# VectorE copies the mixer's R, the last taps, tables and memory are queued later, transposes of queries move by one product, the final scaling runs on three engines

## The chip, the cores and the metric

The kernel runs on one core of a Trainium2 chip, as one launch. The metric is the device time of that launch in microseconds. Engines are named as in the profile: PE is the matrix engine (TensorE), PEld its weight loads, DVE is VectorE, ACT is ScalarE, POOL is GpSimd, and SP (SyncE) issues most DMAs.

## The reference

Two layers over 512 tokens of width 1024, all in float32. Each layer is a half-step SwiGLU FFN (hidden width 2816), a mixer of three groups of heads (gated causal convolution of 31 taps with LayerNorm and silu, sliding-window attention, attention to 256 memory tokens), a second half-step FFN, and a final norm:

```python
for l in range(DEPTH):
    h = x + 0.5 * swiglu(rms_norm(x, ffn1_norm[l]), ffn1_w1[l], ffn1_w3[l], ffn1_w2[l])
    n = rms_norm(h, mix_norm[l])
    u_conv, q, k, v, q_mem = jnp.split(n @ w_in[l], splits, axis=-1)
    y_conv = conv_module(u_conv, conv_w[l], conv_b[l], conv_ln_g[l], conv_ln_b[l])
    q = apply_rope(rms_norm(q, swa_q_norm[l]), cos, sin)
    k = apply_rope(rms_norm(k, swa_k_norm[l]), cos, sin)
    y_swa = sliding_window_attention(q, k, v, swa_sinks[l])
    mk, mv = jnp.split(rms_norm(mem, mem_norm[l]) @ w_mem_kv[l], 2, axis=-1)
    y_mem = memory_attention(rms_norm(q_mem, mem_q_norm[l]), rms_norm(mk, mem_k_norm[l]), mv)
    h = h + jnp.concatenate([y_conv, y_swa, y_mem], axis=-1) @ w_out[l]
    h = h + 0.5 * swiglu(rms_norm(h, ffn2_norm[l]), ffn2_w1[l], ffn2_w3[l], ffn2_w2[l])
    x = rms_norm(h, final_norm[l])
```

## The kernel before

**Layout.** Activations lie transposed: the residual `h` is 8 blocks of 128 channels by 512 tokens. RMS norms need sums over channels, so squares are added up on ACT and DVE, and PE sums them over partitions (`col_sums`, a matmul with a column of ones per 128 tokens); `rms_cols` makes the factor per token (POOL's power in `rsq`), and `spread` turns it into a 128x512 tile `R` with the same value on all partitions, by four matmuls. `kept` copies that tile from PSUM to SBUF.

**Precision by three products.** Every large product is done three times in a reduced format: each operand is split into a high and a low part (`hi`, `lo`), and `mm3` multiplies hi by hi, lo by hi and hi by lo (lines 174 to 176). A weight tile is loaded raw (512 KB for 1024 columns, three `raw` buffers, four `whi`/`wlo` pairs). Then ACT writes hi (line 143) and DVE writes lo as raw minus hi (line 144): that is `split`, one DVE operation of 1.2 us a tile. The other way is `split_by_dma`: ACT writes hi and minus hi (lines 148, 149), and a DMA issued by POOL adds the raw weight from HBM onto it (line 150). `weights(..., on)` chooses: V is the first way, G the second.

**FFN.** `ffn` computes the first four of 22 hidden units plainly (`up`, whose weights are chosen between the two ways), and the others in pairs with a scheme of seven products (`Seven`, `up_pair`), which needs sums of operands and weights on DVE (`msum`, line 298; `raw`, line 363). The hidden units are used in four quarters of 6, 6, 6 and 4; after each, eight output blocks are accumulated and added to `h` (line 460). In the first FFN of a layer, a function `aside` is called after quarter 0: `prepare(l)`, which makes the rope tables (layer 0 only, some sixty small DVE operations, lines 475 to 514), this layer's tables `cg`, `sg` and `gmem` (lines 556 to 559), and the memory tokens' keys and values (`memory`, a product of 48 matmuls with its own weights, operand splits at line 154, and four weight tiles).

**Mixer.** The input projection is a sequence of products, written in a string `ORDER`: `c00` to `c21` are the six halves of the convolution's GLU, `q0` to `q3` the queries and keys of 128 tokens each, `Q0` to `Q3` their transposes to columns, `v`, `V` the same for values and memory queries, `a` the attention, `t0` to `t2` the taps of three blocks of convolution channels (31 DVE operations each), `s` its LayerNorm and swish. Then the output projection has two phases: first the five blocks of attention for all eight outputs, then the three of the convolution. `a` runs the last convolution half inside.

**Order.** Tile's scheduler decides each engine's order of instructions from the program's order, priorities and its own model of time. `tc.issue_after(x)`, used by `queued()`, tells it to place instructions behind x; it adds no semaphore. All engines work through their queues in order, so an instruction that waits holds up what is behind it.

**Tail.** After the last FFN, `spread` of the last factor stays in PSUM, DVE scales eight 128x512 blocks by it and by the final gain (line 975), and SP writes each block out (line 976).

Of the kernel before, what the change touches and what calls it, by code (L numbers as in the profile page):

```python
# [10 lines left out]
F32 = mybir.dt.float32  # L11
# [7 lines left out]
P = 128  # L19
D = 1024  # L20
# [25 lines left out]

ORDER = "c00 c01 q0 c10 q1 Q0 c11 q2 Q1 v0 q3 Q2 v1 v2 Q3 V0 v3 V1 c20 V2 V3 a t0 t1 t2 s"

# [13 lines left out]
def trunk(ctx: ExitStack, tc: tile.TileContext, xT, memT, pos, w1a, w3a, w2a, w1b, w3b, w2b,  # L62
# [131 lines left out]
    def col_sums(st, tag="cf"):  # L194

        ss = bank([P, 4], tag)
        for t in range(st.n // P):
            for i, x in enumerate(st.sums):
                tail[0] = T.matmul(ss[:, t : t + 1], x[:, blk(t)], onec, start=i == 0, stop=i == len(st.sums) - 1)
        return ss  # L200
# [13 lines left out]

    def kept(pr, tag):
        R = res.tile([P, S], F32, tag=tag, name=tag)
        A.activation(R, pr, AF.Copy)
        return R
# [180 lines left out]
    def ffn(l, w13, w2, x, sums, factors, last, at_product, aside=None):  # L399
# [38 lines left out]
        for q, (f0, nf) in enumerate(QUARTERS):  # L438
# [14 lines left out]
            for d in range(KD):  # L453
                while len(begun) < (d + 1 if ahead or d else 3):
                    with nullcontext() if ahead or d else queued():
                        begin(len(begun))
                ps, w = begun[d]
                for j in range(nf - 2, nf):
                    mm3(ps, at(w, ALL, blk(j)), g[f0 + j], False, j == nf - 1)
                V.scalar_tensor_tensor(out=h[:, d, :], in0=ps, scalar=0.5, in1=h[:, d, :], op0=ALU.mult, op1=ALU.add)  # L460
                if not ahead:
                    last(d)
            if aside and not q:
                aside()

# [141 lines left out]
    def mixer(l, x, st, last):  # L607
# [32 lines left out]
        def conv_half(c, i):  # L640
            nonlocal R
            ps = bank([P, S], "po") if c == 2 else mm()
            with queued():
                project(ps, weights(wconv[l, c, i], 1024, G if c else V, spare() if c == 2 else None), x)
            if c == 0:
                with queued():
                    if i == 0:
                        V.tensor_copy(rc, rms_cols(st, D))
# [142 lines left out]
        def scaled(kind, b, po):  # L791
# [10 lines left out]
            z = ring("yn")[:, 0 : n * HD]  # L802
            V.tensor_tensor(out=heads(z), in0=po[:, :, 0:HD], in1=rd.unsqueeze(2).to_broadcast([P, n, HD]), op=ALU.mult)
            return z

        def attended(kind, b, z):
# [58 lines left out]
        def taps(c):  # L865
            V.tensor_scalar(out=cv[:, c, :], in0=ypad[:, c, 0:S], scalar1=conv_w[:, c, 0:1], scalar2=conv_b[:, c : c + 1],
                            op0=ALU.mult, op1=ALU.add)
            for j in range(1, TAPS):
                V.scalar_tensor_tensor(out=cv[:, c, :], in0=ypad[:, c, j : j + S], scalar=conv_w[:, c, j : j + 1],  # L869
                                       in1=cv[:, c, :], op0=ALU.mult, op1=ALU.add)  # L870

# [51 lines left out]
    for l in range(L):  # L923
# [44 lines left out]
        else:  # L968
            def last(d):
                st.add(h[:, d, :], last=d == KD - 1)  # L970

            ffn(l, (w1b, w3b), w2b, nxt.x, sums, factors, last, 1)
            pr = spread(rms_cols(st, D))
            for d in range(KD):
                V.scalar_tensor_tensor(out=h[:, d, :], in0=h[:, d, :], scalar=fin[:, d : d + 1], in1=pr, op0=ALU.mult, op1=ALU.mult)
                nc.sync.dma_start(out[:, d, :], h[:, d, :])
# [58 lines left out]
```

## Time and profile before

| | before |
|---|---|
| time, median of 3 | 1820.17 us (1819.33 to 1820.87) |
| the profiled execution | 1818.45 us |
| its span on the core | 1816.7 us |
| mean granted PE clock | 0.996 |
| DMA traffic | 250.45 MB, mean 138 GB/s |

Each execution's time includes 1.75 us around the span that the profile shows. The page gives the busy time of each engine; the windows give PE's idle time by place. In layer 0 the first FFN runs to about 380 us, the mixer to about 570, and the second FFN follows; layer 1 starts near 910, its mixer near 1270. A row of a timeline has the start, the duration, engine, line, operation, names, shapes, and in brackets the idle time before it and what ended it.

### The profile page before, as it was taken

Reading aid. Unit: us, or ns where it says so; the run is one execution under the profiler, and the core shown is the slowest. Engines: PE = TensorE matmul, PEld = TensorE weight load, DVE = VectorE, ACT = ScalarE, POOL = GpSimd, SP = SyncE. Lnnn points to the kernel's source line nnn. Section 1 sums busy time; section 2 is a strip of 40 time slices with the busy share of each in tenths; the row PEclk is TensorE's granted clock in tenths of the full one; section 3 lists DMA queues with packets and bytes.
Section 4 is the critical chain, followed back from the end, with each engine's and each line's share of the span. In section 5 each row is a group of like instructions: output and inputs, shape, how many; then the busy total and the mean of one; then the engine's idle time right before and its main releaser. Section 6 shows DMA issues by size and latency. Waiting matters only on the chain.

```text
span 1816.7 us, 28098 instructions
## 1 busy us (share of the span) xinstructions
PE 1763.6 (97%) x10996; PEld 1578.3 (87%) x10996; DVE 1281.8 (71%) x1902; ACT 899.6 (50%) x1367; POOL 192.3 (11%) x207
## 2 busy tenths in 40 slices
PE   8999999999999999999999999999989999999997
PEld 6889999878788989898888898988777879898986
DVE  8967666569947857575678675766698567675755
ACT  4545444364746535353655453535456555353532
POOL 2001000025111000000010010000350010000000
PEclk9999999999999999999999999999999999999998
DMA  7456655173148456565565475643640566474622
GB/s 245 109 169 172 169 136 152 53 215 80 36 98 208 107 144 168 142 164 140 155 137 156 144 176 141 169 119 98 170 103 16 146 158 161 131 182 120 167 78 81
DMA packets 93589, 250.45 MB, mean 138 GB/s; under 512 B 9616, under 2 KB 11920, under 8 KB 93456
## 3 DMA queue, kind: packets, MB, share of 16 engines
q1 hardware_dynamic: 77040, 190.45, 34.2%
q0 software_dynamic: 16416, 58.20, 17.7%
q8 instruction: 86, 1.41, 0.3%
q14 instruction: 47, 0.39, 0.1%
HBM read 246.52 MB, written 2.10 MB: 137 GB/s over the span
## 4 chain that ended last, share of the span: by engine, by line
PE 75%; DVE 12%; issue 6%; DMA 4%; ACT 2%; SPq 0%; POOLq 0%; DVEq 0%; POOL 0%; ACTq 0%
PE mm L174 10%; PE mm L175 10%; PE mm L176 10%; PE po L174 8%; PE po L176 8%; PE po L175 8%; PE pt L175 6%; PE pt L174 6%; PE pt L176 6%; DVE there L869 5%; DVE wlo L144 1%; DMA raw<-in_wvm 1%; DMA raw<-in_wconv 1%; DVE nmw L760 1%; PE cf L174 1%
## 5 line engine op out<-in xcount | busy, mean ns | idle before, releaser
L143 ACT ACTIVATE whi<-raw 128x1024 fp32r<-128x1024 f32 (+3 forms) x368 | 339.2, 925 | 481.8 <-PE mm L175 233.4
L144 DVE TENSOR_TENSOR wlo<-raw,whi 128x1024 fp32r<-128x1024 f32 (+3 forms) x368 | 388.9, 1058 | 156.2 <-ACT whi L143 154.9
L175 PE MATMUL mm<-glo,whi 128*128 128x512 f32 x752 | 293.7, 391 | 0.0
L176 PE MATMUL mm<-ghi,wlo 128*128 128x512 f32 x752 | 292.6, 389 | 0.0
L174 PE MATMUL mm<-ghi,whi 128*128 128x512 f32 x752 | 290.8, 391 | 0.7 <-ACT ghi L143 0.7
L176 PE MATMUL po<-mh,wlo 128*128 128x256 f32 x864 | 244.6, 283 | 1.4 <-DVE wlo L144 1.4
L174 PE MATMUL po<-mh,whi 128*128 128x256 f32 x864 | 244.8, 283 | 0.8 <-ACT part L382 0.8
L174 PE MATMUL pt<-xhi,whi 128*128 128x256 f32 x864 | 243.2, 283 | 2.4 <-ACT xhi L143 2.0
L175 PE MATMUL pt<-xlo,whi 128*128 128x256 f32 x864 | 243.8, 283 | 1.5 <-DVE xlo L144 1.5
L175 PE MATMUL po<-ml,whi 128*128 128x256 f32 x864 | 244.6, 283 | 0.0
L176 PE MATMUL pt<-xhi,wlo 128*128 128x256 f32 x864 | 243.7, 283 | 0.0
L460 DVE SCALAR_TENSOR_TENSOR h<-mm,h 128x512 f32<-128x512 f32 x128 | 87.8, 689 | 137.3 <-PE mm L176 137.3
L174 PEld LDWEIGHTS pt<-xhi,whi 128*128 128x128 f32 x864 | 165.1, 192 | 3.9 <-ACT xhi L143 2.4
L175 PEld LDWEIGHTS pt<-xlo,whi 128*128 128x128 f32 x864 | 165.7, 192 | 2.5 <-DVE xlo L144 1.7
L174 PEld LDWEIGHTS mm<-ghi,whi 128*128 128x128 f32 x752 | 141.2, 188 | 30.2 <-ACT ghi L143 1.2
L174 PEld LDWEIGHTS po<-mh,whi 128*128 128x128 f32 x864 | 165.8, 192 | 1.8 <-ACT part L382 1.2
L176 PEld LDWEIGHTS po<-mh,wlo 128*128 128x128 f32 x864 | 165.8, 192 | 1.6 <-DVE wlo L144 1.6
L176 PEld LDWEIGHTS mm<-ghi,wlo 128*128 128x128 f32 x752 | 141.3, 188 | 29.8 <-issue 0.5
L175 PEld LDWEIGHTS po<-ml,whi 128*128 128x128 f32 x864 | 165.8, 192 | 0.6
L175 PEld LDWEIGHTS mm<-glo,whi 128*128 128x128 f32 x752 | 141.3, 188 | 28.3 <-issue 0.5
L176 PEld LDWEIGHTS pt<-xhi,wlo 128*128 128x128 f32 x864 | 165.5, 192 | 0.0
L869 DVE SCALAR_TENSOR_TENSOR there<-ypad,par,there 128x512 f32<-128x512 f32 x180 | 135.7, 762 | 1.4
(304 smaller groups left out, 3280.2 us busy)
## 6 DMA issues: line engine op xcount, KB each, us to landing
raw<-in_w2a SPq DMA_DIRECT2D x48, 384.0 KB, 3.6
raw<-in_w2b SPq DMA_DIRECT2D x48, 384.0 KB, 3.5
raw<-in_w1b SPq DMA_DIRECT2D x26, 512.0 KB, 3.6
raw<-in_w3b SPq DMA_DIRECT2D x26, 512.0 KB, 3.9
raw<-in_w1a SPq DMA_DIRECT2D x25, 512.0 KB, 3.6
raw<-in_w3a SPq DMA_DIRECT2D x25, 512.0 KB, 3.9
wsum<-in_w1a SPq DMA_DIRECT2D x18, 512.0 KB, 4.3
wsum<-in_w3a SPq DMA_DIRECT2D x18, 512.0 KB, 4.4
```

The source lines that it names most:

```text
L143: A.activation(hi, x, AF.Copy)
L144: on.tensor_tensor(out=lo, in0=x, in1=hi.bitcast(F32), op=ALU.subtract)
L174: T.matmul(ps, a[0], b[0], start=first, stop=False, **more)
L175: T.matmul(ps, a[0], b[1], start=False, stop=False, **more)
L176: tail[0] = T.matmul(ps, a[1], b[0], start=False, stop=last, **more)
L460: V.scalar_tensor_tensor(out=h[:, d, :], in0=ps, scalar=0.5, in1=h[:, d, :], op0=ALU.mult, op1=ALU.add)
L760: V.tensor_reduce(out=each(nmw, i), in_=pp[i], axis=AX.X, op=ALU.max)
L869: V.scalar_tensor_tensor(out=cv[:, c, :], in0=ypad[:, c, j : j + S], scalar=conv_w[:, c, j : j + 1], in1=cv[:, c, :], op0=ALU.mult, op1=AL ...
```

## The change

Eight edits in one diff:

1. `ORDER` moves the transposes `Q0`, `Q1`, `Q2` one product later.
2. `col_sums` runs over the partial sums first and over the tokens' blocks inside, so that products of the first partial sum need not wait for the second.
3. In the mixer, DVE instead of ACT copies `R`.
4. In the mixer, half `c10` of the convolution has its weight split on DVE and not by DMA.
5. In layer 0's first FFN, unit 3 of the plain units has its two weights split by DMA and not on DVE.
6. `aside` (tables and memory) is placed behind the eighth addition to `h` of quarter 0.
7. The last ten taps of the last channel block are placed behind the last scaling of window attention.
8. The final scaling: ACT multiplies by the gain as each block of `h` is done, and the factor per token is spread, copied (ACT) and multiplied (DVE) by blocks of 128 tokens for six of the eight channel blocks, with one output DMA each; POOL multiplies the other two.

```diff
-ORDER = "c00 c01 q0 c10 q1 Q0 c11 q2 Q1 v0 q3 Q2 v1 v2 Q3 V0 v3 V1 c20 V2 V3 a t0 t1 t2 s"
+ORDER = "c00 c01 q0 c10 q1 c11 Q0 q2 v0 Q1 q3 v1 Q2 v2 v3 Q3 V0 V1 c20 V2 V3 a t0 t1 t2 s"
...
         ss = bank([P, 4], tag)
-        for t in range(st.n // P):
-            for i, x in enumerate(st.sums):
-                tail[0] = T.matmul(ss[:, t : t + 1], x[:, blk(t)], onec, start=i == 0, stop=i == len(st.sums) - 1)
+
+        for i, x in enumerate(st.sums):
+            for t in range(st.n // P):
+                tail[0] = T.matmul(ss[:, t : t + 1], x[:, blk(t)], onec, start=i == t == 0, stop=i == len(st.sums) - 1, skip_group_check=True)
...
-    def kept(pr, tag):
+    def kept(pr, tag, on=A):
         R = res.tile([P, S], F32, tag=tag, name=tag)
-        A.activation(R, pr, AF.Copy)
+        if on is A:
+            A.activation(R, pr, AF.Copy)
+        else:
+            on.tensor_copy(R, pr)
         return R
...
-            project(ps, weights(w13[i][l, f], 1024, V if f == 0 or l == 0 and w13[0] is w1a else G), x)
+            project(ps, weights(w13[i][l, f], 1024, V if f == 0 or f < 3 and l == 0 and w13[0] is w1a else G), x)
...
-                V.scalar_tensor_tensor(out=h[:, d, :], in0=ps, scalar=0.5, in1=h[:, d, :], op0=ALU.mult, op1=ALU.add)
+                added = V.scalar_tensor_tensor(out=h[:, d, :], in0=ps, scalar=0.5, in1=h[:, d, :], op0=ALU.mult, op1=ALU.add)
                 if not ahead:
                     last(d)
             if aside and not q:
-                aside()
+                with tc.issue_after(added.ins):
+                    aside()
...
-                project(ps, weights(wconv[l, c, i], 1024, G if c else V, spare() if c == 2 else None), x)
+                project(ps, weights(wconv[l, c, i], 1024, V if c + i < 2 else G, spare() if c == 2 else None), x)
...
-                        R = kept(spread(rc), "R")
+                        R = kept(spread(rc), "R", V)
...
-            V.tensor_tensor(out=heads(z), in0=po[:, :, 0:HD], in1=rd.unsqueeze(2).to_broadcast([P, n, HD]), op=ALU.mult)
+            scaling[kind] = V.tensor_tensor(out=heads(z), in0=po[:, :, 0:HD], in1=rd.unsqueeze(2).to_broadcast([P, n, HD]), op=ALU.mult)
...
             for j in range(1, TAPS):
-                V.scalar_tensor_tensor(out=cv[:, c, :], in0=ypad[:, c, j : j + S], scalar=conv_w[:, c, j : j + 1],
-                                       in1=cv[:, c, :], op0=ALU.mult, op1=ALU.add)
+
+                with tc.issue_after(scaling["w"].ins) if c == CC - 1 and j > 2 * TAPS // 3 else nullcontext():
+                    V.scalar_tensor_tensor(out=cv[:, c, :], in0=ypad[:, c, j : j + S], scalar=conv_w[:, c, j : j + 1],
+                                           in1=cv[:, c, :], op0=ALU.mult, op1=ALU.add)
...
                 st.add(h[:, d, :], last=d == KD - 1)
+                A.activation(h[:, d, :], h[:, d, :], AF.Copy, scale=fin[:, d : d + 1])
...
-            pr = spread(rms_cols(st, D))
-            for d in range(KD):
-                V.scalar_tensor_tensor(out=h[:, d, :], in0=h[:, d, :], scalar=fin[:, d : d + 1], in1=pr, op0=ALU.mult, op1=ALU.mult)
+            r = rms_cols(st, D)
+            R = res.tile([P, S], F32, tag="R", name="R")
+            k = KD - 2
+            for t in range(NT):
+                pr = bank([P, P], ("mm", "po")[t % 2])
+                T.matmul(pr, r[:, t : t + 1].to_broadcast([P, P]), ident, start=True, stop=True)
+                A.activation(R[:, blk(t)], pr, AF.Copy)
+                z = h[:, 0:k, blk(t)]
+                V.tensor_tensor(out=z, in0=z, in1=R[:, blk(t)].unsqueeze(1).to_broadcast([P, k, P]), op=ALU.mult)
+                nc.sync.dma_start(out[:, 0:k, blk(t)], z)
+            for d in range(k, KD):
+                G.tensor_tensor(out=h[:, d, :], in0=h[:, d, :], in1=R, op=ALU.mult)
                 nc.sync.dma_start(out[:, d, :], h[:, d, :])
```

The first place is DVE's queue at the end of quarter 0 in layer 0's first FFN. Line 460 (464 in the changed kernel) is the addition to `h`, one for each of eight outputs; lines 154 and 144 with `raw`, `gn` and 128x1024 are memory's operand and weight splits. Before:

```order
L154 SCALAR_TENSOR_TENSOR wlo_1270<-raw_1267,gn_80,whi_1269 128x256 x4
L460 SCALAR_TENSOR_TENSOR h_79<-mm_1134,h_79 128x512
L144 TENSOR_TENSOR wlo_1291<-raw_1292,whi_1290 128x1024
L242 TENSOR_TENSOR st_1273<-st_1273,sq_1332 128x256
L242 TENSOR_TENSOR st_1273<-st_1273,sq_1337 128x256
L242 TENSOR_TENSOR st_1273<-st_1273,sq_1342 128x256
L242 TENSOR_TENSOR st_1273<-st_1273,sq_1347 128x256
L460 SCALAR_TENSOR_TENSOR h_79<-mm_1160,h_79 128x512
L144 TENSOR_TENSOR wlo_1309<-raw_1310,whi_1308 128x1024
L460 SCALAR_TENSOR_TENSOR h_79<-mm_1186,h_79 128x512
L154 SCALAR_TENSOR_TENSOR wlo_1329<-raw_1326,gn_80,whi_1328 128x256 x4
```

and in the changed kernel:

```order
L464 SCALAR_TENSOR_TENSOR h_79<-mm_1162,h_79 128x512
L464 SCALAR_TENSOR_TENSOR h_79<-mm_1188,h_79 128x512
L488 CAST pf_1208<-posi_102 128x4
L565 TENSOR_TENSOR gmem_125<-rw_100 128x64
L154 SCALAR_TENSOR_TENSOR wlo_1272<-raw_1269,gn_80,whi_1271 128x256 x2
L246 TENSOR_TENSOR st_1275<-st_1275,sq_1279 128x256
L154 SCALAR_TENSOR_TENSOR wlo_1272<-raw_1269,gn_80,whi_1271 128x256 x2
L144 TENSOR_TENSOR wlo_1293<-raw_1294,whi_1292 128x1024
L144 TENSOR_TENSOR wlo_1311<-raw_1312,whi_1310 128x1024
L489 TENSOR_TENSOR ypad_108<-cst_96,pf_1208 128x128
```

The first half of memory's splits (`wlo_1270`, `wlo_1291`, `wlo_1309`) stood ahead of the eighth addition; now the same splits (`wlo_1272`, `wlo_1293`, `wlo_1311`) stand behind it, with the rope table's operations after them. In layer 1 the same place of the changed kernel reads:

```order
L464 SCALAR_TENSOR_TENSOR h_79<-mm_9733,h_79 128x512
L561 TENSOR_TENSOR cg_123<-cs_114,rw_100 128x4x64
L563 SCALAR_TENSOR_TENSOR sg_124<-sn_115,rw_100 128x4x32 x2
L561 TENSOR_TENSOR cg_123<-cs_114,rw_100 128x4x64
L563 SCALAR_TENSOR_TENSOR sg_124<-sn_115,rw_100 128x4x32 x2
L565 TENSOR_TENSOR gmem_125<-rw_100 128x64
L154 SCALAR_TENSOR_TENSOR wlo_9765<-raw_9762,gn_80,whi_9764 128x256 x4
L144 TENSOR_TENSOR wlo_9775<-raw_9776,whi_9774 128x1024
```

Layer 1's six table operations, which DVE did during layer 0's mixer before, now stand between the addition and the first split. On PE, the memory product's place has not moved: it follows the quarter's last product directly in both kernels, and in the changed kernel (layer 0) its first instructions are:

```order
L176 MATMUL mm_1188<-ghi_749,wlo_1183 128x512
L174 MATMUL cf_1267<-whi_1292,whi_1271 128x512
L174 MATMUL mm_1268<-whi_1292,whi_1271 128x512
L175 MATMUL cf_1267<-wlo_1293,whi_1271 128x512
L176 MATMUL cf_1267<-whi_1292,wlo_1272 128x512
```

Two of them use high parts only; the third reads `wlo_1293`.

The second place is PE's queue in layer 0's mixer, at the transposes of the first queries (`Q0`, lines 566 and 571, from the tile `query`). Before:

```order
L174 MATMUL mm_3938<-ghi_3857,xhi_3582 128x512
L175 MATMUL mm_3938<-glo_3858,xhi_3582 128x512
L176 MATMUL mm_3938<-ghi_3857,xlo_3583 128x512
L566 MATMUL pt_3979<-cst_96,query_3744 128x128 x4
L174 MATMUL mm_3986<-xhi_3582,whi_3987 128x512
```

and in the changed kernel:

```order
L174 MATMUL mm_3980<-xhi_3584,whi_3981 128x512
L175 MATMUL mm_3980<-xlo_3585,whi_3981 128x512
L176 MATMUL mm_3980<-xhi_3584,wlo_3982 128x512
L571 MATMUL pt_4015<-cst_96,query_3746 128x128 x4
L174 MATMUL mm_4022<-ghi_3838,xhi_3584 128x512
```

The transposes stood behind the product of `q1` and now stand behind the next one, that of `c11`.

The third place is DVE's queue at the end of layer 0's attention; line 869 (878) is a tap, lines 798 to 803 (803 to 808) are the scaling of one block's attention, line 881 (890) begins the swish. Before:

```order
L869 SCALAR_TENSOR_TENSOR there<-ypad,par,there 128x512 x2
L144 TENSOR_TENSOR glo<-pt,ghi 128x128
L746 TENSOR_REDUCE nmr<-mm 128x2
L746 TENSOR_REDUCE nmr<-cf 128x2
L144 TENSOR_TENSOR glo<-pt,ghi 128x2x128
L747 SCALAR_TENSOR_TENSOR nmr<-nmr,rm 128x4
L144 TENSOR_TENSOR glo<-pt,ghi 128x2x128
L798 TENSOR_TENSOR rd_4772<-po,esw 128x2x3
L799 RECIPROCAL rd_4772<-rd_4772 128x6
L803 TENSOR_TENSOR aux_3741<-po,rd_4772 128x384
L801 RECIPROCAL rd_4794<-po 128x4
```

and in the changed kernel:

```order
L808 TENSOR_TENSOR aux_3743<-po,rd_4773 128x384
L878 SCALAR_TENSOR_TENSOR there<-ypad,par,there 128x512 x2
L806 RECIPROCAL rd_4795<-po 128x4
L878 SCALAR_TENSOR_TENSOR there<-ypad,par,there 128x512
L808 TENSOR_TENSOR aux_3743<-po,rd_4795 128x256
L144 TENSOR_TENSOR glo<-pt,ghi 128x128
L878 SCALAR_TENSOR_TENSOR there<-ypad,par,there 128x512
L144 TENSOR_TENSOR glo<-pt,ghi 128x2x128
L878 SCALAR_TENSOR_TENSOR there<-ypad,par,there 128x512
L144 TENSOR_TENSOR glo<-pt,ghi 128x2x128
L878 SCALAR_TENSOR_TENSOR there<-ypad,par,there 128x512 x5
```

Ten taps, which were spread among attention's operations before, come after the last window scaling (384 columns wide), between and behind the last splits of the attention's output.

More of the change, by code (lines that the diff above doesn't have):

```diff
@@ L802, in scaled @@
             z = ring("yn")[:, 0 : n * HD]
-            V.tensor_tensor(out=heads(z), in0=po[:, :, 0:HD], in1=rd.unsqueeze(2).to_broadcast([P, n, HD]), op=ALU.mult)
+            scaling[kind] = V.tensor_tensor(out=heads(z), in0=po[:, :, 0:HD], in1=rd.unsqueeze(2).to_broadcast([P, n, HD]), op=ALU.mult)
             return z
+        scaling = {}
         def attended(kind, b, z):
```

## The prediction

> **What bounds the kernel now.** I read the page first for who is busy, then its chain, then the matrix engine's waits, then windows around the waits.
>
> ```profile
> PE 1763.6 (97%) x10996; PEld 1578.3 (87%) x10996; DVE 1281.8 (71%) x1902; ACT 899.6 (50%) x1367; POOL 192.3 (11%) x207
> ...
> PE 75%; DVE 12%; issue 6%; DMA 4%; ACT 2%; SPq 0%; POOLq 0%; DVEq 0%; POOL 0%; ACTq 0%
> ```
>
> PE is the bound: 1763.6 of the span's 1816.7 us. The change adds and removes no large product, so only the 53.1 us in which PE stands still, and stretches at a low clock, are to be won. In the chain that ended last DVE is the next engine with 12%. So the reader is to look for where PE's idle time lies, and what DVE did before it.
>
> ```profile
> 60.00:80.00 20.00, 16.51 (x135) 1.00 0.62 167
> 130.00:150.00 20.00, 20.00 (x105) 1.00 0.42 132
> ...
> 380.00:510.00 130.00, 117.92 (x690) 0.99 0.36 88
> ...
> 1270.00:1410.00 140.00, 127.49 (x737) 1.00 0.40 98
> 1800.00:1816.70 16.70, 5.30 (x31) 0.67 0.34 126
> ```
>
> In each window the columns are its length, PE's busy time, the granted clock, DMA's share and GB/s. The two mixers hold 12.1 and 12.5 us of idle time, the first FFN's start 3.5, the tail 11.4. Between 130 and 150, where the memory tokens are projected in layer 0, PE never stops; that row matters below. The waits say who ended the idle time (total, count, longest).
>
> ```profile
> PE pt L566 <- DVE query L542: 5.0, 4, 1.3
> PE cf L176 <- DMA wlo<-in_wconv: 3.2, 2, 1.6
> PE pt L566 <- DVE query L690: 3.0, 2, 1.5
> ...
> PE pt L174 <- ACT xhi L143: 2.0, 1, 2.0
> PE pt L175 <- DVE xlo L144: 1.5, 1, 1.5
> PE cf L199 <- ACT sq L230: 1.4, 1, 1.4
> ```
>
> **First FFN, layer 0.** The waits of 2.0 and 1.5 us are both in the window 60 to 80: ACT and PE wait for sums that DVE makes late.
>
> ```profile
> 69.22 1.28 DVE L298 TENSOR_TENSOR msum<-n 128x512 f32<-128x512 f32 x2
> ```
>
> DVE has no gap around it. Among what it does before are the rope table's small operations and the fourth unit's weight splits:
>
> ```profile
> L144 DVE TENSOR_TENSOR wlo<-raw,whi 128x1024 fp32r<-128x1024 f32 x9 | 10.8, 1213 | 0.0
> ...
> L480 DVE SCALAR_TENSOR_TENSOR ypad<-ypad 128x128 f32<-128x128 f32 x4 | 1.1, 280 | 0.0
> ```
>
> The order of the changed kernel has no rope operation in this stretch, and the two splits of the fourth unit go to ACT with an accumulating DMA. Two splits at 1.2 and about ten small operations at 0.2 to 0.28 take some 4.5 us off DVE ahead of the sum, more than the 3.5 us of stall. **Gain 3.5**, bounds 2 to 3.5. The way by DMA is longer, and hidden by an early load:
>
> ```profile
> 34.22 1.06 ACT L143 ACTIVATE whi<-raw 128x1024 fp32r<-128x1024 f32 x1 [2.54 <-DMA raw<-in_w1a]
> ```
> ```profile
> 47.23 0.39 PE L174 MATMUL mm<-xhi,whi 128*128 128x512 f32 x1
> ```
>
> The fourth unit's first tile is there at 34.2, and PE comes to it at 47.2: 13 us for two copies of 1.06, an issue of 0.9 and a landing. Without that cover the loss would be like the 1.6 of the convolution's wait above.
>
> **Memory projection, both layers: the new wait.** `aside` is now queued behind the eighth h addition of quarter 0 (the first pieces of the order above). Before, its weight splits ran while PE was still in the quarter's last products:
>
> ```profile
> 132.14 1.22 DVE L144 TENSOR_TENSOR wlo<-raw,whi 128x1024 fp32r<-128x1024 f32 x1
> 135.34 0.69 DVE L460 SCALAR_TENSOR_TENSOR h<-mm,h 128x512 f32<-128x512 f32 x1 [1.98 <-PE mm L176]
> 135.94 1.66 DVE L154 SCALAR_TENSOR_TENSOR wlo<-raw,gn,whi 128x256 fp32r<-128x256 f32 x4
> ```
> ```profile
> 134.91 0.39 PE L176 MATMUL mm<-ghi,wlo 128*128 128x512 f32 x1
> 135.14 0.39 PE L174 MATMUL cf<-whi 128*128 128x512 f32 x1
> 135.37 0.39 PE L175 MATMUL cf<-wlo,whi 128*128 128x512 f32 x1
> ```
>
> PE went from the quarter's last product (134.91) into the memory product (135.14) without a gap, and its second instruction already reads a wlo. In the changed order PE still does exactly this, but now that wlo's split stands behind the h addition, which itself waits for the last product. From the addition's start DVE needs 0.60 (start to start, 135.34 to 135.94), some 0.3 for two small operations, 1.66 for the four scaled splits, one square sum (about 0.4) and 1.22 for the weight: the wlo is there 4.2 us after 135.34. PE can do two matmuls that need no wlo, until 135.6. It waits about 4.0. Then memory's second half: DVE has the rope's small operations between, about 7.1 us of work from the first weight's split to the third's, against 5.4 us of PE work (24 matmuls at 0.227 from start to start): 1.7 more. Layer 0 pays 5.7. In layer 1 there is no rope, but six table operations stand ahead of the splits, which the trace shows in the mixer:
>
> ```profile
> 440.24 0.28 DVE L558 SCALAR_TENSOR_TENSOR sg<-sn,rw 128x128 f32<-128x128 f32 x1
> ...
> 441.18 0.41 DVE L556 TENSOR_TENSOR cg<-cs,rw 128x256 f32<-128x256 f32 x1
> ```
>
> Two of 0.33 and four of 0.2 from start to start are 1.5 us in place of the square sum and the cast, so the first wait is about 4.8. The second half's raw tiles can only load when the first half's are split, which adds about half a microsecond: 5.2. **Loss 10.9 together.** Bounds 8 (only the first waits, DVE's small operations overlapping better) and 15 (below). Afterwards DVE has about 70 us of work in the next quarter's 76 us of PE time, so the lag is worked off without a second stall.
>
> PE's clock may fall after such a gap. The trace has this once:
>
> ```profile
> 433.29 0.44 PE L566 MATMUL pt<-cst,query 128*128 128x128 f32 x1 [1.24 <-DVE query L542]
> ...
> 434.50 0.52 PE L174 MATMUL mm<-whi,xhi 128*128 128x384 f32 x1
> ...
> 437.98 0.33 PE L176 MATMUL mm<-whi,xlo 128*128 128x384 f32 x1
> ```
> ```profile
> 434.00:435.00 1.00, 1.00 (x5) 1.00 (x4) 1.00 (x2) 0.43 (x2) 0.93 (x1) 0.50 0.91 160
> ```
>
> After gaps of 1.53 and 1.24 us the clock was 0.50 and a matmul took 0.52 instead of 0.33, for some 3.4 us: 1.7 lost. Layer 1 has the same two gaps (1.51, 1.25) with the clock at 1.00, and so has 60 to 80 with 3.5 us of idle time. I count no drop in the sum, and keep 1.7 per layer as a bound. The Trainium skill, "TensorE: Matmul & The Clock Gate", Part 1, says that the clock halves after an idle window of about 3.4 us whose position is free-running, and recovers after a busy one. By that rule a 4-us gap would often be long enough, and the sum would be 3.4 us worse if both were hit; the one drop above came at shorter gaps, so the trace and the rule agree only in the length of the recovery.
>
> **Mixer, both layers.** Four edits.
>
> ```profile
> 387.83 0.92 POOL L150 DMA_DIRECT2D wlo<-in_wconv  x1 [2.37 <-ACT wlo L149]
> ```
> ```profile
> 385.49 0.17 DVE L648 COPY rc<-rsq 128x4 f32<-128x4 f32 x1 [1.98 <-POOL rsq L191]
> 394.67 0.96 DVE L144 TENSOR_TENSOR wlo<-raw,whi 128x768 fp32r<-128x768 f32 x1 [9.01 <-ACT whi L143]
> ```
>
> The accumulating DMA issued at 387.83 is what PE waits 1.6 us for. Splitting that weight on DVE, idle for 9.0 us there, takes 1.22 and removes the wait: 1.6 per layer. The split stands ahead of the copy of rc, which moves from 385.5 to about 388.0; its first reader is PE's spread of rc at 388.73, so 0.7 is left, and the price without that cover is what the split is late. R's copy costs DVE 0.6, ahead of the first gates.
>
> The queries' transposes wait 8.0 us in all, 4.0 per layer, for DVE's L690 and L542. One product later is 24 matmuls, 4 to 5 us, more than the longest sum of two waits (2.8). They should nearly go, and with them layer 0's slow clock (1.7). But DVE has no gap from 398 to 504, so a PE that runs ahead meets DVE further on:
>
> ```profile
> 398.00:504.00 106.00, 103.40 (x202) 0.98 0.26 62
> ```
> ```profile
> L869 DVE SCALAR_TENSOR_TENSOR there<-ypad,par,there 128x512 f32<-128x512 f32 x90 | 67.7, 761 | 0.7
> ```
>
> Hence the mixer's gain is the smaller of two sums. PE's: 1.6 + 4.0, 1.7 in layer 0, and something of the 6 us of idle time left in attention. DVE's: ten taps put behind the last scaling (about 0.70 from start to start, 7.0 us), tables out in layer 0 (1.5), less 1.2 and 0.6 for the new split and copy: 6.7 and 5.2. The deferred taps then lie beside the output projection's first phase, 120 matmuls or 27 us; their reader, the convolution's swish, has to be done by its end, and seven us of taps fit. I take **6.5 and 5.5**, bounds 3 to 9 each.
>
> **Tail.**
>
> ```profile
> 1804.65 0.16 DVE L205 TENSOR_SCALAR ms<-cf 128x4 f32<-128x4 f32 x1 [2.54 <-PE cf L199]
> 1808.10 5.35 DVE L975 SCALAR_TENSOR_TENSOR h<-h,gn,pt 128x512 f32<-128x512 f32 x8 [3.28 <-PE pt L212]
> ```
> ```profile
> 1808.87 4.94 SPq L976 DMA_DIRECT2D out<-h  x8
> ```
> ```profile
> 501.43 0.28 ACT L143 ACTIVATE ghi<-pt 128x128 fp32r<-128x128 f32 x1
> ```
>
> Half of the column sums no longer stand behind the last square (1.4 wait): 0.8 earlier. The scaling starts after one spread block, not four, with an ACT copy of 128x128 between (about 0.3, by the row of that shape) and a 128x768 multiplication (about 0.87, between 0.41 for 256 and 1.21 for 1024 columns): the first output leaves near 1807.4 instead of 1808.87. All is issued within 3.5 us, less than the old queue's 4.94, so the 7.8 us from the first issue to the span's end should follow as before: 1.5 gained at the old rate. The new output rows have 512 bytes instead of 2048, a kind the trace doesn't show; if they cost double, 2.6 are lost. I take **gain 1**, near the old rate. "DMA: Bandwidth & Descriptors" of the Trainium skill (Specifications) names 512 bytes as enough for full rate, by which the gain would be the 1.5; no run here shows it.
>
> **Sum.** -3.5 + 10.9 - 6.5 - 5.5 - 1.0 = -5.6 us. The profiled execution took 1818.45 (span 1816.7), so 1812.8 by it; the median of the runs shown, 1820.17, is 1.7 above, so I forecast 1814.6.
>
> **Rivals.**
> 1. *The memory wait is mostly hidden.* That needs a free DVE at the eighth addition. Against it: the order, and PE's second matmul that needs wlo. For it: nothing but room for overlap. With 3 instead of 10.9: -13.5, 1806.7. Chance 0.15.
> 2. *DVE keeps the mixer.* The transposes' waits go, and PE loses the same time in attention; only the convolution's wait and a little are won, 3 per layer: -3.5 + 10.9 - 6 - 1 = +0.4, 1820.6. For it: DVE's unbroken row. Chance 0.22.
> 3. *Slower: the memory wait is longer than the split's own row.* Its second half shares three raw tiles; each load (3.6 us to landing by the row below) starts only when DVE has freed one, then ACT takes 1.0 and DVE 1.2. If this turnaround sets the pace, plus the clock's 1.7, a layer pays 9 to 10 and the sum becomes -16.5 + 19.5 = +3, with the mixer's gain one microsecond short per layer +5: 1825. It decides from about 10 per layer. For it: the gap begins with all buffers waiting on DVE. Chance 0.16.
> ```profile
> raw<-in_w1a SPq DMA_DIRECT2D x25, 512.0 KB, 3.6
> ```
>
> 4. Forecast: 0.47.
>
> A measurement of this kernel tells about 0.2% (3.6 us) from no change. Faster by more: all of 1 and nine tenths of 4, 0.57; slower: 3 and a little of 2, 0.18; within: 0.25. The range takes in rival 1 in most of its width and rival 2, with the mixer's and the memory's bounds: 1804 to 1824.
>
> **What would show it.** Right: PE idle 4 to 6 us behind quarter 0's last product in both layers, released by DVE wlo (lines 144 and 154), in rows that read 20.00 of 20.00 before; the waits on `query` nearly gone; 60 to 80 full; no wait for a DMA of wlo from in_wconv; idle time in both mixers about half. Wrong: no gap at the memory's products (rival 1); idle time in attention grown by what the transposes won (rival 2); gaps of 8 us or a granted clock of 0.5 behind them (rival 3); outputs whose packets go on for longer than 7.8 us after the first issue.

## The result and the profile after

| | before | after |
|---|---|---|
| time, median | 1820.15 us (1819.33 to 1820.87) | 1844.72 us (1842.64 to 1846.07) |
| ratio of the times, 95% interval | | 1.0134 [1.0117, 1.0152] |
| the profiled execution / its span | 1818.45 / 1816.7 us | 1842.64 / 1840.9 us |
| mean granted PE clock | 0.996 | 0.987 |

The change makes the kernel 1.3% slower; I had forecast 0.3% faster. From the page of the changed kernel, the busy times and the chain by engine:

```profile
PE 1777.9 (97%) x10996; PEld 1588.1 (86%) x10996; DVE 1283.8 (70%) x1900; ACT 903.4 (49%) x1377; POOL 191.9 (10%) x209
...
PE 79%; DVE 13%; DMA 4%; ACT 3%; issue 1%; DVEq 0%; SPq 0%; POOL 0%; ACTq 0%
```

PE has the same 10996 instructions and is busy 14.3 us longer, and it stands still for 63.0 us (1840.9 - 1777.9) instead of 53.1. So of the 24.2 us that the span grew, 10 are new waiting and 14 are longer matmuls. The clock accounts for them: ahead of the tail, the stretches with a granted clock of 0.50 cost 1.7 us before and 16.4 after (half of PE's busy time in them). The additions to `h` show where. Each row is the start of the last one of a stage, from the timeline of DVE in both kernels, and the last column what the stage added to the difference:

| last h addition of | before | after | step |
|---|---|---|---|
| layer 0, first FFN, quarter 0 | 135.34 | 131.22 | -4.1 |
| layer 0, first FFN, quarter 1 (behind the memory product) | 240.34 | 244.72 | +8.5 |
| layer 0, first FFN, quarter 3 | 376.20 | 380.58 | 0.0 |
| layer 0, mixer | 558.39 | 563.68 | +0.9 |
| layer 0, second FFN, quarter 0 | 677.28 | 686.09 | +3.5 |
| layer 1, first FFN, quarter 0 | 1031.14 | 1039.55 | -0.4 |
| layer 1, first FFN, quarter 1 (behind the memory product) | 1135.64 | 1151.57 | +7.5 |
| layer 1, mixer | 1452.66 | 1472.08 | +3.5 |
| layer 1, second FFN, quarter 0 | 1572.96 | 1596.42 | +4.0 |
| layer 1, second FFN, quarter 3 | 1801.43 | 1824.90 | 0.0 |
| end of the span | 1816.7 | 1840.9 | +0.7 |

Stages that are left out add nothing. Windows of 20 us of the changed kernel at these places (length, PE's busy time, granted clock, DMA's share and GB/s):

```profile
120.00:140.00 20.00, 16.41 (x66) 0.91 0.23 71
...
560.00:580.00 20.00, 14.88 (x61) 0.91 0.81 212
...
1040.00:1060.00 20.00, 15.38 (x65) 0.83 0.48 157
...
1360.00:1380.00 20.00, 16.61 (x93) 0.91 0.32 64
...
1460.00:1480.00 20.00, 14.77 (x62) 1.00 0.80 223
```

Each place has both: 3.4 to 5.2 us in which PE isn't busy, and a clock below 1.00 (at the last, the slow stretch falls into the next window). And its waits, which answer to those of before:

```profile
PE cf L175 <- DVE wlo L144: 9.2, 3, 4.7
...
PE cf L200 <- DVE st L246: 5.2, 3, 2.2
PE po L174 <- DVE ypad L665: 5.1, 2, 2.6
...
PE pt L571 <- DVE query L547: 0.6, 2, 0.3
```

The wait for the accumulating DMA is gone, and of 8.0 us for `query` 0.6 are left. New are the wait at the memory product (`cf`), one of the last convolution half for the gate of the half before (`ypad`), and those for the squares at the start of the second FFN (`st`: two of 2.2 us; before, one of 1.1 in all).

**The memory product**, from PE's timeline in layer 0, and the windows behind it:

```profile
131.25 0.39 PE L174 MATMUL mm<-whi 128*128 128x512 f32 x1
135.22 0.67 PE L175 MATMUL cf<-wlo,whi 128*128 128x512 f32 x1 [3.58 <-DVE wlo L144]
135.69 0.63 PE L176 MATMUL cf<-whi,wlo 128*128 128x512 f32 x1
```
```profile
136.00:137.00 1.00, 1.00 (x4) 0.71 (x4) 1.00 (x5) 0.00 (x0) 0.00 (x0) 0.50 0.86 336
```

PE does the two matmuls without a wlo, waits 3.58 us for the split, and then runs at a clock of 0.50 for about 3.4 us: 0.63 us for a matmul that takes 0.39.

**The end of the mixer.** DVE's additions of the output projection, before and after:

```profile
543.34 0.69 DVE L907 TENSOR_TENSOR h<-mm,h 128x512 f32<-128x512 f32 x1 [1.15 <-PE mm L176]
...
545.49 0.68 DVE L907 TENSOR_TENSOR h<-mm,h 128x512 f32<-128x512 f32 x1
...
547.64 0.68 DVE L907 TENSOR_TENSOR h<-mm,h 128x512 f32<-128x512 f32 x1
```
```profile
549.85 0.69 DVE L916 TENSOR_TENSOR h<-mm,h 128x512 f32<-128x512 f32 x1 [5.01 <-PE mm L176]
...
550.92 0.69 DVE L916 TENSOR_TENSOR h<-mm,h 128x512 f32<-128x512 f32 x1
...
551.99 0.68 DVE L916 TENSOR_TENSOR h<-mm,h 128x512 f32<-128x512 f32 x1
```

Before, PE finished one block every 2.15 us and DVE followed at that pace. Now DVE is idle for 5 us and then gets blocks as fast as it can take them: PE finishes the products with the convolution's last part at the end of the phase, for several blocks together. The first addition is 6.5 us later (4.9 of them since the projection's first product), and with it the operand splits and squares that the second FFN begins with, so PE waits there:

```profile
571.27 1.05 PE L200 MATMUL cf<-onesq,st 128*128 128x1 f32 x8 [2.15 <-DVE st L246]
572.19 0.68 PE L174 MATMUL mm<-xhi,whi 128*128 128x512 f32 x1
```

### The profile page after: what moved, and what is told of

It is laid out like the page before. It is cut to its first block, busy times and chain, and to the rows that moved or that the text cites. A ratio compares the mean times of both kernels' runs of the same rounds, so it can differ in the third digit from the quotient of the medians.

```text
span 1840.9 us, 28100 instructions
## 1 busy us (share of the span) xinstructions
PE 1777.9 (97%) x10996; PEld 1588.1 (86%) x10996; DVE 1283.8 (70%) x1900; ACT 903.4 (49%) x1377; POOL 191.9 (10%) x209
## 4 chain that ended last, share of the span: by engine, by line
PE 79%; DVE 13%; DMA 4%; ACT 3%; issue 1%; DVEq 0%; SPq 0%; POOL 0%; ACTq 0%
PE mm L174 11%; PE mm L175 11%; PE mm L176 11%; PE po L174 9%; PE po L176 8%; PE po L175 8%; PE pt L174 6%; PE pt L175 6%; PE pt L176 6%; DVE there L878 6%; DVE wlo L144 1%; DMA raw<-in_wconv 1%; DMA raw<-in_wvm 1%; DVE nmw L765 1%; ACT whi L143 1%
## 5 line engine op out<-in xcount | busy, mean ns | idle before, releaser
L143 ACT ACTIVATE whi<-raw 128x1024 fp32r<-128x1024 f32 (+4 forms) x368 | 338.9, 925 | 510.8 <-PE mm L175 257.4
L144 DVE TENSOR_TENSOR wlo<-raw,whi 128x1024 fp32r<-128x1024 f32 (+4 forms) x368 | 388.6, 1058 | 168.9 <-ACT whi L143 168.1
```

Source lines behind the costliest of these rows:

```text
L143: A.activation(hi, x, AF.Copy)
L144: on.tensor_tensor(out=lo, in0=x, in1=hi.bitcast(F32), op=ALU.subtract)
```

## The experiments

Twelve kernels, all with the whole computation. The time of before is measured anew with each group: 1820.6 with the first four, 1821.4 with the next four, 1821.8 and 1820.6 with the rest. "The split order" below stands for the edit in `ffn` and `prepare` that leaves rope and tables behind the eighth addition and lets the memory projection go free.

**1. Tables and memory free again** (the changed kernel otherwise).

```diff
-                with tc.issue_after(added.ins):
-                    aside()
+                aside()
```


> The changed kernel, with the tables and the memory projection no longer placed behind the eighth h addition. Theory M (that placement costs two waits at the memory product and the slow clock behind them, 8.5 us in layer 0 and 7.5 in layer 1 by the landmarks): 1844.7 - 16 = about 1829, PE full from the last product of quarter 0 on, granted clock 1.00 there, and the 3.5 us stall of layer 0's first FFN may come back in part (up to 1832). Rival (the time is lost elsewhere and only shows up here): above 1838.

Measured 1836.09 (1.0083 [1.0067, 1.0099]). The memory product's quarter took what it took before in both layers (steps of 0.0 instead of +8.5 and +7.5). But most of the 4.1 us won in layer 0's first FFN went too (+0.5 at the end of quarter 0), since the rope's operations stand in it again: PE waits 1.9 us for ACT's `part`. Not all of it is the rope: a stretch at half clock at 25.6 us cost this execution 1.7, and run 4, with the same edit and no such stretch, kept 1.3 of the 4.1. So the placement does both: it removes one stall and makes another. The gain fell short of the 16 us expected, by time neither theory nor rival. The profile shows where: the mixers took 3.6 and 2.7 us longer than in the changed kernel (steps of +4.5 and +6.2), with 6.1 and 5.1 us of half clock on the way to the projection's first product instead of 3.4 and 1.7.

**2. Taps not deferred.**

```diff
-                with tc.issue_after(scaling["w"].ins) if c == CC - 1 and j > 2 * TAPS // 3 else nullcontext():
+                with tc.issue_after(scaling["w"].ins) if False else nullcontext():
```


> The changed kernel, with the last ten taps no longer deferred. Theory T (the deferral makes the convolution's output late, the second phase of the output projection finishes all eight blocks in a bunch, DVE is then late for the second FFN: 5 us of waits and 1.7 us of slow clock in layer 0, about the same in layer 1): 1844.7 - 10 = about 1835, with the wait of 2.2 us for the sum of squares at the start of the second FFN back to near 0. Rival (DVE's total work sets the mixer, the taps cost the same wherever they stand): 1843 to 1847, with the idle time back in attention.

Measured 1829.46 (1.0046 [1.0031, 1.0061]): 15 us faster than the change. The steps of the second FFN's start are +0.2 and -0.8 instead of +3.5 and +4.0, those of the mixers -1.9 and +2.3 instead of +0.9 and +3.5. Of the three edits taken back singly this one gives most, more than the 10 us expected, and its term had been forecast as a gain.

**3. The order string of before.** (Beside `Q0` to `Q2` the new string also moves `Q3` and `V0`, behind `v3`.)

```diff
-ORDER = "c00 c01 q0 c10 q1 c11 Q0 q2 v0 Q1 q3 v1 Q2 v2 v3 Q3 V0 V1 c20 V2 V3 a t0 t1 t2 s"
+ORDER = "c00 c01 q0 c10 q1 Q0 c11 q2 Q1 v0 q3 Q2 v1 v2 Q3 V0 v3 V1 c20 V2 V3 a t0 t1 t2 s"
```


> The changed kernel with the order string of before. Theory D (DVE's queue sets the mixer's pace: the transposes' waits that the new string removes come back as waits for the gate of c20 and c21): within 3 us of 1844.7, the 4 us of waits for query back, the 2.5 us wait for the gate gone. Rival (the string itself costs the mixer its 3 to 4 us): 1836 to 1838. Rival (the string gains what was forecast): 1850.

Measured 1840.32 (1.0109 [1.009, 1.0129]), between theory and rival. The waits for `query` are back (5.3 us), those for the gate are gone; the mixers are a little shorter by the steps (-0.9 and +0.2 instead of +0.9 and +3.5).

**4. Both 1 and 2.** 

> The changed kernel without the placement of tables and memory and without the deferral of taps. If M and T hold and add up: 1844.7 - 16 - 10 = about 1819, the time of before within 3 us, or a little under it. If something else in the change costs time: 1825 or more.

Measured 1821.76 (1.0006 [0.9994, 1.0018]): the two losses add up to the whole difference, and what is left of the change can't be told from nothing in sum.

**5. Taps and order as before, and the split order.** (Of the edits only the split order is printed.)

```diff
                 with tc.issue_after(added.ins):
-                    aside()
+                    aside[0]()
+                aside[1]()
...
-        memory(l)
...
-        ffn(l, (w1a, w3a), w2a, x, sums, factors, into(gn[:, l, N_MIX], (st, None)), 2, lambda: prepare(l))
+        ffn(l, (w1a, w3a), w2a, x, sums, factors, into(gn[:, l, N_MIX], (st, None)), 2, (lambda: prepare(l), lambda: memory(l)))
```


> The changed kernel with three things set back: the taps are not deferred, the order string is that of before, and of what was placed behind the eighth h addition only the rope and table operations stay there, while the memory projection is free again. If the three causes found so far are all there is: the first FFN keeps its 4.2 us of gain, the memory product has no wait (0), the mixers keep the early split of c10 (about 2 to 3 us in all): 1820.6 - 9 = about 1811. Rival (the rope operations in the next quarter push other splits late): a wait there, 1815 to 1820. Rival (slow clock somewhere else): 1816 or more.

Measured 1818.31 (0.9984 [0.9967, 1.0001]). The gain of 4.2 us in the first FFN stays and the memory product costs 0.0 in both layers, as expected. But single executions lie between 1811.89 and 1826.56, with mean granted clocks of 0.995 and 0.985: the expected 1811 is the time of the one execution in which the clock hardly fell. By the median it is the rival, slow clock elsewhere: the profiled execution, the slowest of the ten, has 10.2 us at half clock from 498.5 on and six more such stretches ahead of the tail.

**6. The same with the new order string.** 

> The same, but with the new order string. If the string costs by DVE's queue (the waits for the gates of c20 and c21 take the place of the transposes' waits, with a slow clock behind the longer one), this is slower than its neighbour by some 4 us, about 1816. If the string gains what was forecast it is faster by 3 to 6: 1806.

Measured 1814.61 (0.9961 [0.9945, 0.9977]), faster than before. Against run 5 the ranges overlap, so the string's own worth isn't settled; in this pair it didn't cost. The 3.7 us between them go with the clock: the median of the granted clock is 0.993 here and 0.990 in run 5.

**7. Only the deferral, on the kernel before.** 

> The kernel before with one edit, the deferral of the last ten taps. Theory T: 1820.6 + 12 = about 1832, with the bunched h additions at the end of the output projection and the waits at the start of the second FFN. Forecast of the prediction's step (the deferral gains DVE time in attention): 1816. Rival (it only costs together with the new order string): 1820.

Measured 1831.99 (1.0057 [1.0038, 1.0075]): theory T. It costs without the new string too.

**8. Only the split of c10 on DVE and the copy of R on DVE, on the kernel before.** 

> The kernel before with two edits, c10's weight split on DVE and R copied by DVE. The prediction's step: the waits of 1.6 us for the accumulating DMA go in both layers, 1820.6 - 3.2 = 1817.4. Rival (DVE sets the mixer's pace further on, so that the time is lost again before the end of attention): 1820 to 1821, with no wait for in_wconv but more for query.

Measured 1821.36 (1.0001 [0.9986, 1.0017]): the rival by time, but not by its sign. The DMA's wait is gone, and the waits for `query` didn't grow: they are 6.1 us instead of 8.0. Between the first FFN's end and the first product of the output projection PE's idle time fell from 12.1 and 12.5 us to 9.6 and 9.6. That stretch still takes 134.3 and 132.7 us where the kernel before needs 133.6 and 132.6, since half clock costs 5.5 and 4.1 us in it instead of 1.7 and 0. The profiled execution is 3.7 us above the median, but the ten agree: the median of their granted clock is 0.9905, and 0.994 for the kernel before. So the profile shows the time lost to the clock, and not again in waiting for DVE.

**9. Run 6, with a free PSUM bank for the last convolution half.**

```diff
-                to_columns(qmT[:, :, blk(t)], scratch[0][:, blk(t, 256)], 2, "po")
+                to_columns(qmT[:, :, blk(t)], scratch[0][:, blk(t, 256)], 2, "pt")
```


> The faster variant so far (memory free, rope and tables behind the eighth addition, taps not deferred, new order string), with one edit: the transposes of the memory queries use the tag pt and not po, so that the product of c21 finds a free po bank and need not wait for DVE's gate of c20, which stands behind seven taps. If that wait (2.9 and 2.8 us, each with a slow clock of 1.6 to 2.6 us behind it) is what the new string left in the mixer: 4 to 5 us per layer, 1814.6 - 9 = about 1806, no wait of PE po for ypad. Rival (DVE sets the mixer's end): the wait moves into attention, 1813 to 1815.

Measured 1817.71 (0.998 [0.996, 0.9999]), no better than run 6. The waits of run 6 and of this run, from their lists of PE's waits:

```profile
PE po L174 <- DVE ypad L665: 5.7, 2, 2.9
PE pt L783 <- ACT uu L777: 3.5, 4, 0.9
```
```profile
PE pt L783 <- ACT uu L777: 7.0, 6, 2.2
PE po L794 <- ACT aux L785: 3.9, 3, 2.0
```

The wait for the gate is gone, and attention's waits for the softmax have grown by 6.1 us. What they stand behind is mostly ACT. ACT's timeline at the first two of the new waits:

```profile
454.25 1.28 ACT L777 ACT_TABLE_LOAD   x1 [7.63 <-DVE nmr L752]
455.55 1.93 ACT L777 ACTIVATE uu<-mm,nmr,rm 128x256 f32<-128x256 f32 x4
457.49 1.28 ACT L669 ACT_TABLE_LOAD   x1
```

PE stands idle from 453.95 to 456.16. DVE's last operation for the maxima ends at 454.15; the rest is a load of ACT's function table (1.28 us, between the sigmoid of the gates and the exponential of the softmax) and the first exponential. Each of the four new waits over 1 us (2.2, 1.7, 1.3 and 2.0) holds such a load or its end. In run 6 ACT makes the same loads beside the last convolution half, where PE doesn't wait for them. PE's idle time up to the projection still fell, from 10.8 and 10.9 us to 10.0 and 9.5, and half clock costs 7.7 and 4.2 us there instead of 3.0 and 1.7.

**10. Run 6, with five taps deferred.**

```diff
-                with tc.issue_after(scaling["w"].ins) if False else nullcontext():
+                with tc.issue_after(scaling["w"].ins) if c == CC - 1 and j > 2 * TAPS // 3 + 5 else nullcontext():
```


> The same faster variant, with five taps deferred instead of none. If the price comes from the late convolution output (second phase finishing in a bunch): five taps are 3.5 us less late than ten, so between none and ten: the whole deferral cost 11 to 15 us, five 3 to 8: 1818 to 1822. If deferral helps attention up to a point: 1812 or less.

Measured 1827.03 (1.0026 [1.0007, 1.0044]), 12 us more than without. Five cost about what ten cost: the price isn't in proportion to the taps' time.

**11. Run 6, with output rows of 1024 bytes.** The final scaling goes by blocks of 256 tokens, three channel blocks each.

```diff
-            for t in range(NT):
+            for t in range(NT // 2):
...
+                for j in range(0, k, 3):
+                    z = h[:, j : j + 3, b]
+                    V.tensor_tensor(out=z, in0=z, in1=R[:, b].unsqueeze(1).to_broadcast([P, 3, 256]), op=ALU.mult)
+                    nc.sync.dma_start(out[:, j : j + 3, b], z)
```


> The same faster variant, with the final scaling in two blocks of 256 tokens and three channel blocks each, so that an output row has 1024 bytes and not 512. If the rows' size made the output slower (285 GB/s against 365 to 410 before): from the last h addition to the end 16.0 becomes 14.5 to 15 us, DMA at 330 GB/s or more, time 1 us less, 1813.6. Rival (POOL's share ends last, row size does not matter): 16 us as it is.

Measured 1813.84 (0.9955 [0.9936, 0.9974]), the fastest kernel of this study, though not told apart from run 6. The trace shows the rows' part: DMA moved some 345 GB/s here against some 290 in run 6, and the end came 15.3 us after the last addition instead of 15.7. That this made the median shorter isn't shown.

**12. The ten taps deferred, memory free, and PE's order in the second phase held.**

```diff
-                mm3(oo[d], at(w, ALL, blk(n)), y[n], False, n == CC - 1)
+                with queued():
+                    mm3(oo[d], at(w, ALL, blk(n)), y[n], False, n == CC - 1)
```


> Memory free, rope and tables behind the eighth addition, new order string, and the ten taps deferred as in the change; one new edit: in the second phase of the output projection each block's three products are kept in the program's order, block by block, by placing each behind the one before. If the deferral's price is the order in which PE finishes the eight blocks (all last products at the end, so that DVE gets eight additions in a bunch): the h additions come 2 us apart again, the second FFN's start has no wait of 2.2 us, PE waits 1 to 3 us once for the last part of the convolution, and attention keeps its gain: 1811 to 1816 (the variant without deferral measured 1814). If the price is DVE's late work as such, whatever PE's order: 1823 to 1828, as with five deferred taps (1827).

Measured 1823.76 (1.0024 [1.0009, 1.004]), which by time is the rival. By place both have a share. DVE's additions of this run in layer 0:

```profile
538.63 0.69 DVE L917 TENSOR_TENSOR h<-mm,h 128x512 f32<-128x512 f32 x1 [0.83 <-PE mm L176]
...
540.78 0.68 DVE L917 TENSOR_TENSOR h<-mm,h 128x512 f32<-128x512 f32 x1
...
542.93 0.68 DVE L917 TENSOR_TENSOR h<-mm,h 128x512 f32<-128x512 f32 x1
```

They are 2.15 us apart again. The intervals between the stages, read from the timelines (first FFN's last addition to the output projection's first product; from there to the first addition; from the projection's first product to the last addition of the second FFN's quarter 0; layer 0 / layer 1):

| kernel | to the projection | to the first addition | to quarter 0's end |
|---|---|---|---|
| before | 133.6 / 132.6 | 33.5 / 33.5 | 167.5 / 168.8 |
| the change | 130.8 / 130.8 | 38.4 / 40.0 | 174.7 / 178.2 |
| run 2, no deferral | 131.7 / 134.9 | 33.5 / 33.5 | 167.7 / 168.1 |
| run 7, only deferral | 132.4 / 131.0 | 40.0 / 40.0 | 177.7 / 178.4 |
| run 6, no deferral | 133.0 / 132.0 | 33.5 / 33.5 | 167.5 / 168.2 |
| run 10, five taps | 131.5 / 131.1 | 38.1 / 38.0 | 175.9 / 176.0 |
| run 12, order held | 130.8 / 133.2 | 35.9 / 35.8 | 171.8 / 172.3 |

Every kernel with a deferral and a free order needs 174 to 178 us from the projection's first product to quarter 0's end, and those without need 167.5 to 170.6 (run 5, whose profiled execution fell to the slow clock there, 171.0 and 173.3). With the order held it is 172. Without the half-clock stretches (half of PE's busy time in them) the groups are cleaner: 167.4 to 169.9 us without a deferral, 172.6 to 173.3 with one and a free order, 170.1 and 170.6 with the order held. So about half of the deferral's price is the order in which PE finishes the blocks. The other half is the lateness itself, 2.4 us until the first addition; run 12 has 1.7 us of half clock in each layer on top. Its profiled execution lost time elsewhere too: in layer 1 it waited 4.3 us for the gate of c20.

## Why the prediction was wrong

- **First FFN, layer 0** (forecast -3.5): right, -4.1. Runs 1 and 4 show that most of it hangs on the rope's place: with the rope free again PE waits 1.9 us there, and run 4 keeps 1.3 of the gain.
- **Memory product** (forecast +5.7 and +5.2): the wait is where and what I said. In layer 0 it was 3.58 and 0.98, with two of 0.30 and 0.44 later, together 5.3. In layer 1 it was one of 4.7. **The term that was mis-sized is the clock, counted as 0.** It fell behind both waits and cost 1.7 and 2.8 us, and the steps were 8.5 and 7.5 (1.5 of layer 0's are neither wait nor slow clock, and stay open). Run 5 shows that the cost is that of memory alone: with its splits free and the rope behind, 0.0 in both layers.
- **Clock.** I argued from one fall in three similar places. In the changed kernel's trace, after the start, a stretch of slow matmuls follows every wait of 2 us or more. The Trainium skill's rule that I weighed ("TensorE: Matmul & The Clock Gate", Part 1: an idle window of about 3.4 us) would have given the right sign for the 3.6 and 4.7 us waits by their length, but waits of 2.15 to 2.6 us were enough here.
- **Mixer to the output projection** (forecast -6.5 and -5.5): -2.8 and -1.8. The waits for `query` and for the DMA went as forecast, but PE's idle time fell by only 3.5 and 2.8 us, and half clock cost 1.7 us more in each layer, where layer 0 was to be rid of it. Part of what was won came back as another wait, as in rival 2. PE came early to the last convolution halves, whose gate stands behind seven taps in DVE's queue. The timelines of DVE and PE in layer 0:

```profile
453.48 5.48 DVE L878 SCALAR_TENSOR_TENSOR there<-ypad,par,there 128x512 f32<-128x512 f32 x7
458.87 0.68 DVE L665 TENSOR_TENSOR ypad<-po,R 128x512 f32<-128x512 f32 x1
```
```profile
459.61 0.78 PE L174 MATMUL po<-xhi,ghi 128*128 128x512 f32 x1 [2.52 <-DVE ypad L665]
460.19 0.63 PE L175 MATMUL po<-xlo,ghi 128*128 128x512 f32 x1
```

  c20's product had ended near 454.9; its gate was done at 459.5. The next half waited 2.52 us for the bank, and then ran slowly. Runs 8 and 9 show that this isn't DVE's queue alone: run 8 has less idle time and less speed, and in run 9 ACT's table loads take the place of the gate.
- **Deferred taps** ("seven us of taps fit", forecast 0 behind the projection's start): **the step that failed**, +7.2 and +9.4 us from the projection's first product to quarter 0's end. I asked only that the swish be done by the first phase's end, said that seven us fit, and didn't read the slack. DVE's last split of the swish, and PE's first product of the second phase, before and after:

```profile
537.55 0.69 DVE L144 TENSOR_TENSOR glo<-aux,ghi 128x512 fp32r<-128x512 f32 x1 [1.08 <-ACT ghi L143]
541.10 0.39 PE L174 MATMUL mm<-ghi,whi 128*128 128x512 f32 x1
```
```profile
544.14 0.69 DVE L144 TENSOR_TENSOR glo<-aux,ghi 128x512 fp32r<-128x512 f32 x1
543.07 0.62 PE L174 MATMUL mm<-ghi,whi 128*128 128x512 f32 x2
```

  Before, the split ended 2.9 us ahead of the second phase; in the changed kernel it ends 1.8 us behind its start. Nor did I ask in which order the scheduler would then let PE finish the blocks, although the order of the changed kernel was there to be read, nor what DVE has to do for each finished block before the next FFN can start. Runs 2, 7 and 10 show the cost, run 12 that about half of it goes with the order. Why five late taps change the scheduler's order as much as ten is not shown.
- **Tail** (forecast -1): +0.7. The first output left 5.97 us after the last addition instead of 7.44, the 1.5 that I had worked out. But rows of 512 bytes went at about 290 GB/s where rows of 2048 had gone at about 380; run 11's rows of 1024 bytes reached 345. The doubling that I took as the far end didn't happen, but the Trainium skill's figure that 512 bytes are enough for full rate ("DMA: Bandwidth & Descriptors", Specifications) doesn't hold for this output.
- **The sum.** With the measured steps: -4.1 + 8.5 + 7.5 + (0.9 + 3.5) + (3.5 + 4.0) - 0.4 + 0.7 = 24.1, against -5.6. The mixers and what follows them missed by 24 (forecast -12, measured +11.9), the memory product by 5. The sign that I gave 0.18 came about mostly by other causes than rival 3: the raw tiles' turnaround could only stand behind layer 0's later waits (1.7 us), layer 1 had none of these, and the clock that rival 3 counted too gave 4.5 of the memory product's 16.0.

## What to carry to other kernels

Where one engine is busy 97% of the time, a change is priced by the waits it makes on that engine, and each of 2 us or more by a second price for the clock behind it (1.6 to 3.4 us in 28 of the 29 cases here). An operation moved behind another on a busy queue has to be followed to the last engine that reads it, and to the order in which the scheduler then finishes things; that it fits into a phase isn't enough. An `issue_after` around a function that holds two kinds of work places both: splitting it (rope behind, memory free) kept the gain and took away the loss.

## What the runs showed of the hardware

- **The slow clock is bought by short waits.** In the fourteen traces, 29 of 31 waits of PE of 2 us or more (outside the first 40 us and the tail) were followed within 5 us by a window with a granted clock below 0.95, and 28 of 86 between 1.2 and 2 us.
- **It falls on a raster.** In each trace the stretches at 0.50 ahead of the tail start on one raster of 3.41 us and last 3.41 us, or two, three or (once) five times that. A single one cost 1.6 to 1.7 us, a double one 2.5 to 3.4 (half of PE's busy time in it).
- **What counts is the slot, not the one wait.** I count, slot by slot of that raster, the time in which PE is idle or has only matmuls of one column (128x1). Of 6006 slots at full clock with less than 1.0 us of it none was followed by a slow slot, of 150 with 1.0 to 1.8 us 22 were, and of 50 with 1.8 us or more 47. This also covers falls without a long wait: in the changed kernel one began at 388.0, after waits of only 0.50 and 0.28 us, and the slot ahead of it has 1.6 us of such time, half of it matmuls of one column. The limits are read off these traces; no run was made to test them.
- **It differs from execution to execution of one kernel.** Run 5's ten executions reach from 1811.89 to 1826.56 us, and the mean granted clock goes with them, from 0.995 to 0.985. A few us between two medians can be the clock alone; for causes the steps between stages were the better measure.
- **A table load of ACT can stand behind a wait of PE.** It took 1.28 us each time; in run 9 four of PE's waits ended on work that stood behind one.
